# Up-projection of a two-layer encoder trunk as seven half-width products instead of eight, with the down-projection in groups of four

## The chip, the core and the metric

One core of a Trainium2 chip runs the whole program. The metric is device time in microseconds; the kernel before was timed three times (1096.11, 1097.59 and 1097.9 us, median 1097.59). One more execution was recorded by the profiler; all durations here come from that one.

## What is computed

Two layers (DEPTH = 2) over 512 positions of 1024 features. Each layer has an attention part and a channel mixer. The change is in the mixer:

```python
h = rms_norm(x, ffn_norm_g[i]) @ w_up[i]          # 1024 -> 2 x 2816
h = depthwise_conv(h, conv_w[i], conv_b[i])       # width 3 over positions
gate, up = jnp.split(h, 2, axis=-1)
x = x + (jax.nn.silu(gate) * up) @ w_down[i]      # 2816 -> 1024
```

## The kernel before

Everything is held feature-major: tiles have 128 features on the partitions and the 512 positions along the free dimension. Products keep fp32 accuracy by splitting each factor into a rounded part (hi) and a remainder (lo) and adding three TensorE products, hi·hi, hi·lo and lo·hi (`mm3`, lines 259 to 262). Weights stream through `WStream`: a chunk of 128x1024 is loaded by SyncE into one of 4 raw buffers; ScalarE writes the rounded half (line 123) and the negated chunk (line 125); a DMA issued by GpSimd (line 126) adds the chunk to that, which leaves the remainder. Six split buffers hold the results; the stream splits 3 plan entries ahead of use and loads 6 ahead.

In the mixer the 22 "pairs" j are 128 gate columns and the matching 128 value columns. `up(j)` (line 648) runs 2 x 8 x 3 = 48 matmuls of 512 columns into two PSUM banks, upg and upv. The rms factor of the positions is applied afterwards: after pair 0 the row statistics are summed on TensorE (`row_rsqrt`, line 232), VectorE computes the inverse root in small steps, and in the middle of pair 1 `row_broadcast` (line 248) spreads it over the partitions; ScalarE copies it out as rb (line 250). Only then can `up_post` (line 664) of pair 0 run: VectorE multiplies each bank by rb (line 670), ScalarE forms the middle tap (672), VectorE adds the outer taps (673 and 675), ScalarE the SiLU (678), VectorE the product (679), and the result g is split (683, 684). `down(g)` (line 687) multiplies a group of finished pairs by w_down, 24 matmuls of 512 columns for each pair, and VectorE adds each bank to x (709). Groups have 8, 8, 4 and 2 pairs (`ffn_order`); the last two stand at the end.

The framework orders each engine's queue once, when the program is built; at run time every queue is strictly in order, and an instruction that waits holds up all behind it. Tiles come from pools with a fixed number of buffers, so a full pool is a wait too.

Of the kernel before, what the change touches and what calls it, by code (L numbers as in the profile page):

```python
# [17 lines left out]
P = 128  # L18
# [6 lines left out]
NH = 8  # L25
# [4 lines left out]
GROUPS = [8, 8, 4, 2]  # L30
GCOLS = [256, 256, 512, 1024]
RAW_BUFS, SPL_BUFS, K8_BUFS, K2_BUFS = 4, 6, 8, 25
# [17 lines left out]
def ffn_order():  # L50
    order = []
    ng = len(GROUPS)
    for g in range(ng):
        lo = sum(GROUPS[:g])
        for j in range(lo, lo + GROUPS[g]):
            order.append(("up", j))
            if g > 0 and j == lo + 1 and g < ng - 1:
                order.append(("dn", g - 1))
    order.append(("dn", ng - 2))
    order.append(("dn", ng - 1))  # L60
    return order


def chunk_plan():
    plan = []
    for l in range(DEPTH):
# [6 lines left out]
        for kind, i in ffn_order():  # L73
            if kind == "up":
                plan += [(("up", l, i, h), 1024) for h in range(2)]
            else:
# [9 lines left out]
class WStream:  # L86
    def __init__(self, nc, wdram, raw_pool, split_pool, ahead_load, ahead_split):
        self.nc, self.w = nc, wdram
        self.raw_pool, self.split_pool = raw_pool, split_pool
# [9 lines left out]
    def chunk(self, i):  # L99
        o, n = self.offs[i] * P, PLAN[i][1]  # L100
        return self.w[o:o + n * P].rearrange("(p n) -> p n", p=P)

    def load_to(self, n):
        while self.loaded < min(n, len(PLAN)):
            i = self.loaded
            n_el = PLAN[i][1]
            t = self.raw_pool.tile([P, CH], F32, name="wraw")
            self.nc.sync.dma_start(out=t[:, 0:n_el], in_=self.chunk(i))
            self.raw[i] = t
            self.loaded += 1  # L110

    def split_to(self, n):
        nc = self.nc
        while self.split < min(n, len(PLAN)):
            i = self.split
            key, n_el = PLAN[i]
            raw = self.raw.pop(i)
            t = self.split_pool.tile([P, 2, CH], F32R, name="wspl")
            pieces = 2 if i == 0 else 1
            st = n_el // pieces  # L120
            for a in range(0, n_el, st):
                e = slice(a, a + st)
                nc.scalar.activation(out=t[:, 0, e], in_=raw[:, e], func=AF.Copy)  # L123
                if key[0] in DMA_LO:
                    nc.scalar.activation(out=t[:, 1, e], in_=raw[:, e], func=AF.Copy, scale=-1.0)  # L125
                    nc.gpsimd.dma_start(out=t[:, 1, e].bitcast(F32), in_=raw[:, e], accum_op=ALU.add)  # L126
                    continue
                lo = nc.gpsimd if key[0] in POOL_LO else nc.vector
                lo.tensor_tensor(out=t[:, 1, e], in0=raw[:, e], in1=t[:, 0, e].bitcast(F32), op=ALU.subtract)
            self.spl[i] = t  # L130
# [18 lines left out]
DMA_LO = ("vv", "u", "a2", "ws", "so", "ao", "up", "dn")  # L149
# [3 lines left out]
def trunk_kernel(ctx: ExitStack, tc: tile.TileContext, xT, wts, pk, gq, rope, out):  # L153
# [6 lines left out]
    splp = ctx.enter_context(tc.tile_pool(name="splp", bufs=SPL_BUFS))  # L160
    k8p = ctx.enter_context(tc.tile_pool(name="k8p", bufs=K8_BUFS))
# [25 lines left out]
    ws = WStream(nc, wts, rawp, splp, ahead_load=AHEAD_LOAD, ahead_split=AHEAD_SPLIT)  # L187
# [79 lines left out]
    for l in range(DEPTH):  # L267
# [98 lines left out]
        qt = [None, None]  # L366
        qs = [None] * NH

        def q_stacks(pi, bank):
            for par in range(2):  # L370
                h = 2 * pi + par
                if h % 4 == 0:
                    qt[h // 4] = k8("qs", F32R)
                a, o = (lohalf, hihalf) if par == 0 else (hihalf, lohalf)
                st = qt[h // 4][:, h % 4]
# [4 lines left out]
        def k_stacks(bank):  # L380
            kt_ = k8("kk", F32R)
            res = []
            for par in range(2):
                a, o = (lohalf, hihalf) if par == 0 else (hihalf, lohalf)
                kh, kl = kt_[:, 2 * par], kt_[:, 2 * par + 1]
# [8 lines left out]
        def vv_stat():  # L394
            vvg = vvx["g"]
            ss = tn(NT * NH, "ssv")
            for b in range(NT):
                sq = k2("sq")
                A.activation(out=sq, in_=vvg[:, b], func=AF.Square)
# [6 lines left out]
        def vv_norm(b):  # L406
            vvg, rs, vh, vl = vvx["g"], vvx["r"], vvx["h"], vvx["l"]
            V.tensor_tensor(out=vvg[:, b].rearrange("p (h d) -> p h d", h=NH), in0=vvg[:, b].rearrange("p (h d) -> p h d", h=NH),
                            in1=rs[:, b * NH:(b + 1) * NH].unsqueeze(2).to_broadcast([P, NH, HD]), op=ALU.mult)
            G.tensor_tensor(out=vvg[:, b], in0=vvg[:, b], in1=sgn_bc, op=ALU.mult)  # L410
            A.activation(out=vh[:, b], in_=vvg[:, b], func=AF.Copy)
# [48 lines left out]
        def scores(h, b):  # L460
# [13 lines left out]
            pt[b] = p  # L474

        ats = []
        att = [None]
        asq = [None]
        pair = []

# [333 lines left out]
```

## Time and profile before

| | us |
|---|---|
| median of three runs | 1097.59 |
| profiled execution, its time | 1096.55 |
| its span | 1094.8 |
| TensorE (PE) busy | 1079.2 (99%) |
| ScalarE (ACT) busy | 657.0 (60%) |
| VectorE (DVE) busy | 602.5 (55%) |
| GpSimd (POOL) busy | 282.0 (26%) |

The mixer of layer 1 fills about 191 to 550 us of the span, that of layer 2 about 731 to 1093 us. A busy time is the sum of the durations of an engine's instructions; successive ones overlap a little, so the distance from start to start of two neighbours is what a queue of them costs. In the rows below "idle" is how long an engine stood still just before an instruction, and the arrow names what it waited for. The profile's lines number the kernel before; in the changed kernel the same code stands about 45 to 130 lines further down.

### The profile page before, as it was taken

The page shows a single profiled execution, that of the slowest core. Times are in us where ns is not written, and L with a number is a line of the kernel's source. Part 1 is how long each engine was busy: PE and PEld are TensorE (multiplying, and loading weights), DVE is VectorE, ACT ScalarE, POOL GpSimd, SP SyncE. Part 2 cuts the span into 40 slices and gives each one's busy share as a digit, 9 for nine tenths or more (in the row PEclk, how much of TensorE's full clock was granted, in tenths as well). Part 3 has the DMA queues.
Part 4 walks back from the last instruction along what each step waited for, and adds up shares of the span by engine and source line. Part 5 has one row for each costly group of instructions (what it writes and reads, how often), then busy time and mean ns, then how long its engine had stood idle before and what let it go on. Part 6 is the DMA issues. An engine that isn't in the chain of part 4 may idle for free.

```text
span 1094.8 us, 13707 instructions
## 1 busy us (share of the span) xinstructions
PE 1079.2 (99%) x5024; PEld 896.8 (82%) x5024; DVE 602.5 (55%) x1068; ACT 657.0 (60%) x928; POOL 282.0 (26%) x335
## 2 busy tenths in 40 slices
PE   8989999999999999999999999999999999999998
PEld 7868888888888888888888878888888888888887
DVE  6678996565521555125647799866545134541353
ACT  7579786666644665346366896686665446563550
POOL 6434623311111111111063444251111111111110
PEclk9999999999999999999999999999999999999999
DMA  7985317888888888887668650377878787878762
GB/s 261 256 206 122 71 22 174 209 206 184 205 187 200 183 201 186 199 188 197 165 158 201 153 134 21 74 189 187 205 197 189 201 190 195 194 197 198 186 140 77
DMA packets 53923, 188.94 MB, mean 173 GB/s; under 512 B 6112, under 2 KB 6752, under 8 KB 53856
## 3 DMA queue, kind: packets, MB, share of 16 engines
q0 software_dynamic: 24480, 89.14, 45.2%
q1 hardware_dynamic: 29088, 98.79, 25.7%
q8 instruction: 39, 0.64, 0.2%
q14 instruction: 28, 0.23, 0.1%
q10 hardware_dynamic: 288, 0.14, 0.0%
HBM read 96.82 MB, written 2.10 MB: 90 GB/s over the span
## 4 chain that ended last, share of the span: by engine, by line
PE 90%; ACT 3%; DVE 3%; issue 1%; POOL 1%; DMA 0%; SPq 0%; DVEq 0%; ACTq 0%; POOLq 0%
PE upg L260 7%; PE upv L261 7%; PE upg L262 7%; PE upg L261 7%; PE upv L262 7%; PE dn L260 7%; PE dn L262 7%; PE upv L260 7%; PE dn L261 7%; PE a L260 1%; PE a L261 1%; PE a L262 1%; PE pT L490 1%; PE ao L261 1%; PE ao L262 1%
## 5 line engine op out<-in xcount | busy, mean ns | idle before, releaser
L126 POOL DMA_DIRECT2D wspl<-wraw x170 | 146.9, 866 | 669.1 <-ACT wspl L125 376.7
L123 ACT ACTIVATE wspl<-wraw 128x1024 fp32r<-128x1024 f32 (+1 forms) x179 | 188.6, 1053 | 203.0 <-issue 57.5
L125 ACT ACTIVATE wspl<-wraw 128x1024 fp32r<-128x1024 f32 x170 | 177.9, 1046 | 0.0
L260 PE MATMUL upg<-xh,wspl 128*128 128x512 f32 x352 | 137.2, 390 | 0.0
L262 PE MATMUL upg<-xh,wspl 128*128 128x512 f32 x352 | 137.0, 389 | 0.0
L262 PE MATMUL upv<-xh,wspl 128*128 128x512 f32 x352 | 137.0, 389 | 0.0
L261 PE MATMUL upv<-xl,wspl 128*128 128x512 f32 x352 | 137.0, 389 | 0.0
L262 PE MATMUL dn<-g,wspl 128*128 128x512 f32 x352 | 137.0, 389 | 0.0
L260 PE MATMUL upv<-xh,wspl 128*128 128x512 f32 x352 | 137.0, 389 | 0.0
L261 PE MATMUL upg<-xl,wspl 128*128 128x512 f32 x352 | 137.0, 389 | 0.0
L261 PE MATMUL dn<-g,wspl 128*128 128x512 f32 x352 | 137.0, 389 | 0.0
L260 PE MATMUL dn<-g,wspl 128*128 128x512 f32 x352 | 136.9, 389 | 0.0
L709 DVE TENSOR_TENSOR x<-x,dn 128x512 f32<-128x512 f32 x63 | 43.0, 686 | 155.3 <-PE dn L262 155.3
L672 ACT ACTIVATE ht<-ht,pk_sb 128x512 f32<-128x512 f32 x88 | 70.6, 807 | 67.8 <-DVE ht L670 67.8
L673 DVE SCALAR_TENSOR_TENSOR ht<-ht,pk_sb 128x511 f32<-128x511 f32 x88 | 65.9, 751 | 81.1 <-ACT ht L672 81.1
L670 DVE TENSOR_TENSOR ht<-upv,rb 128x512 f32<-128x512 f32 x44 | 30.4, 691 | 87.5 <-PE upv L262 87.2
L261 PEld LDWEIGHTS upv<-xl,wspl 128*128 128x128 f32 x352 | 66.1, 188 | 13.8
L262 PEld LDWEIGHTS upg<-xh,wspl 128*128 128x128 f32 x352 | 66.0, 188 | 13.8
L260 PEld LDWEIGHTS upg<-xh,wspl 128*128 128x128 f32 x352 | 66.2, 188 | 13.7
L262 PEld LDWEIGHTS upv<-xh,wspl 128*128 128x128 f32 x352 | 66.1, 188 | 13.7
L262 PEld LDWEIGHTS dn<-g,wspl 128*128 128x128 f32 x352 | 66.1, 188 | 13.7
L261 PEld LDWEIGHTS dn<-g,wspl 128*128 128x128 f32 x352 | 66.1, 188 | 13.7
(199 smaller groups left out, 2009.2 us busy)
## 6 DMA issues: line engine op xcount, KB each, us to landing
wraw<-in_wts SPq DMA_DIRECT2D x177, 512.0 KB, 4.3
wspl<-wraw POOLq DMA_DIRECT2D x170, 512.0 KB, 5.0
x<-in_xT SPq DMA_DIRECT2D x8, 256.0 KB, 6.1
out_y<-x SPq DMA_DIRECT2D x7, 256.0 KB, 2.0
wraw<-in_wts SPq DMA_DIRECT2D x2, 256.0 KB, 3.9
sgn<-in_gq SPq DMA_DIRECT2D x2, 256.0 KB, 4.5
rope<-in_rope SPq DMA_DIRECT2D x2, 256.0 KB, 4.0
pk_sb<-in_pk SPq DMA_DIRECT2D x1, 208.0 KB, 7.2
```

The source lines that it names most:

```text
L123: nc.scalar.activation(out=t[:, 0, e], in_=raw[:, e], func=AF.Copy)
L125: nc.scalar.activation(out=t[:, 1, e], in_=raw[:, e], func=AF.Copy, scale=-1.0)
L126: nc.gpsimd.dma_start(out=t[:, 1, e].bitcast(F32), in_=raw[:, e], accum_op=ALU.add)
L260: T.matmul(out, lhsT=lh, rhs=rh, start=start, stop=False)
L261: T.matmul(out, lhsT=lh, rhs=rl, start=False, stop=False)
L262: T.matmul(out, lhsT=ll, rhs=rh, start=False, stop=stop)
L490: T.transpose(bank[:, b * P:(b + 1) * P], pt[b][:, s * P:(s + 1) * P], ident)
L670: V.tensor_tensor(out=h, in0=banks[i], in1=rb[0], op=ALU.mult)
L672: A.activation(out=tt, in_=h, func=AF.Identity, scale=col(PK_CW + 2 * NCT + ct), bias=col(PK_CB + ct))
L673: V.scalar_tensor_tensor(out=tt[:, 1:S], in0=h[:, 0:S - 1], scalar=col(PK_CW + ct), in1=tt[:, 1:S], op0=ALU.mult, op1=ALU.add)
L709: V.tensor_tensor(out=x_sb[dt], in0=x_sb[dt], in1=bank, op=ALU.add)
```

## The change

Pairs 0 and 1 stay plain. From pair 2 on the gate and value columns of a pair, the even and odd feature tiles, and the first and second half of the positions form a 2 x 2 x 2 block product, done by a Strassen scheme in seven products of half width instead of eight. A product is 4 feature tiles x 3 matmuls = 12 matmuls of 256 columns.

The right factors (`side`, for all four tile pairs kp) are built once in each layer out of the normalised x, by sums and differences of halves, each split into hi and lo: 28 tiles of 128x512. The weight factors are built for each pair from two raw chunks: four sums or differences of 128x512 on VectorE (new lines 153, 154, 155 and 163), then the splits, of which that of chunk A has its remainder made by VectorE (141) instead of by the DMA, and the fourth factor's too. Work on a pair is in four stages on TensorE: A and B (two products each, into the halves of one bank), C (one product added to the half bank of A) and D (two products into the bank of B); the order is C(j), A(j+1), D(j), B(j+1). Shared sums come from ScalarE copies `pc` of banks A and B, taken before C and D write into them again, and from five 128x256 additions on VectorE.

The down-projection has groups of 4, 4, 4, 4, 4 and 2 pairs; the first four run between pairs, the last two at the end. Many four-in-one tiles become single ones (8 and 25 buffers become 3 and 45), two buffers for weight sums are added, and GpSimd's DMA scratch is set to 8192 bytes.

```diff
-GROUPS = [8, 8, 4, 2]
-GCOLS = [256, 256, 512, 1024]
-RAW_BUFS, SPL_BUFS, K8_BUFS, K2_BUFS = 4, 6, 8, 25
+GROUPS = [4, 4, 4, 4, 4, 2]
+GCOLS = [512, 512, 512, 512, 512, 1024]
+J0 = 2
+RAW_BUFS, SPL_BUFS, CMB_BUFS, K8_BUFS, K2_BUFS = 4, 6, 2, 3, 45
...
+            if key[0] == "upA":
+                r0, r1 = self.raw.pop(i)
+                lo, hi = slice(0, 512), slice(512, 1024)
+                c = self.cmb_pool.tile([P, CH], F32, name="wcmb")
+                V.tensor_tensor(out=c[:, lo], in0=r0[:, lo], in1=r0[:, hi], op=ALU.subtract)
+                V.tensor_tensor(out=c[:, hi], in0=r0[:, hi], in1=r1[:, hi], op=ALU.add)
+                V.tensor_tensor(out=r0[:, hi], in0=c[:, hi], in1=r0[:, lo], op=ALU.subtract)
+                self.pair[key[1:]] = (r0, r1, c)
+                self.spl[i] = self.halves(r0, slice(0, CH), key)
+            elif key[0] == "upB":
+                self.spl[i] = self.halves(self.pair[key[1:]][2], slice(0, CH), key)
+            elif key[0] == "upC":
+                r0, r1, _ = self.pair.pop(key[1:])
+                s4 = self.k2("s4")
+                V.tensor_tensor(out=s4, in0=r1[:, 0:512], in1=r0[:, 512:1024], op=ALU.subtract)
+                four = self.halves(s4, None, key, out=(self.k2("s4h", F32R), self.k2("s4l", F32R)), dma=False)
+                self.spl[i] = (self.halves(r1, slice(0, CH), key), four)
...
                 if j == 1 and n == KT - 1:
                     rb[0] = row_broadcast(rf[0])
-                    up_post(0, held[0])
+                    up_post(0, scaled(held[0]))
+                    for kp in range(KT // 2):
+                        side(kp)
...
+        def side(kp):
+
+            e, o = k2("zx"), k2("zx")
+            for t, d in ((e, 2 * kp), (o, 2 * kp + 1)):
+                V.scalar_tensor_tensor(out=t, in0=x_sb[d], scalar=col(PK_FN + d), in1=rb[0], op0=ALU.mult, op1=ALU.mult)
+            ta, tb = k2("zt"), k2("zt")
+            V.tensor_tensor(out=ta[:, lo2], in0=e[:, lo2], in1=e[:, hi2], op=ALU.subtract)
+            G.tensor_tensor(out=ta[:, hi2], in0=o[:, lo2], in1=e[:, lo2], op=ALU.subtract)
+            V.tensor_tensor(out=tb[:, lo2], in0=o[:, lo2], in1=ta[:, lo2], op=ALU.subtract)
+            G.tensor_tensor(out=tb[:, hi2], in0=o[:, hi2], in1=tb[:, lo2], op=ALU.subtract)
+            u = unit("ze")
+            parts = [(e[:, hi2], u[:, lo2], u[:, hi2])] + [(t, unit("zh"), unit("zl")) for t in (o, ta, tb)]
+            for t, h, w in parts:
+                A.activation(out=h, in_=t, func=AF.Copy)
+                V.tensor_tensor(out=w, in0=t, in1=h.bitcast(F32), op=ALU.subtract)
...
+        def product(out, hi, lo, z, first, last):
+            for kp in range(KT // 2):
+                sl = slice(kp * P, (kp + 1) * P)
+                rh, rl = Z[kp][z]
+                for n, (w, r) in enumerate(((hi, rh), (hi, rl), (lo, rh))):
+                    T.matmul(out, lhsT=w[:, sl], rhs=r, start=first and kp == 0 and n == 0,
+                             stop=last and kp == KT // 2 - 1 and n == 2, skip_group_check=True)
...
+        def stage(kind, j):
+            if kind in "AB":
...
+                product(bank[:, lo2], w[:, 0, 0:512], w[:, 1, 0:512], p0, True, False)
+                product(bank[:, hi2], w[:, 0, 512:1024], w[:, 1, 512:1024], p1, False, True)
+                c = k2("pc")
+                A.activation(out=c, in_=bank, func=AF.Copy)
...
+            elif kind == "C":
...
+                product(bank[:, lo2], w[:, 0, 0:512], w[:, 1, 0:512], "B21", False, True)
+                val = pairs[j]["val"] = k2("h")
+                A.activation(out=val[:, hi2], in_=bank[:, lo2], func=AF.Copy)
...
+                product(bank[:, lo2], w[:, 0, 512:1024], w[:, 1, 512:1024], "T4", False, False)
+                product(bank[:, hi2], four[0], four[1], "B22", False, True)
+                V.tensor_tensor(out=p["gate"][:, hi2], in0=bank[:, lo2], in1=u[:, lo2], op=ALU.add)
+                V.tensor_tensor(out=p["val"][:, lo2], in0=bank[:, hi2], in1=u[:, lo2], op=ALU.add)
+                up_post(j, [p["gate"], p["val"]])
```

Three places show what stands in a queue before and now. The first is VectorE in layer 1 from the spread of the row factor to the end of pair 0 (diag is the input of the spread, ht and g the tiles of `up_post`, L709 the multiplication by rb that was L670). Before:

```order
L246 TENSOR_TENSOR diag<-ident,rl 128x512
L670 TENSOR_TENSOR ht<-upg,rb 128x512
L670 TENSOR_TENSOR ht<-upv,rb 128x512
L673 SCALAR_TENSOR_TENSOR ht<-ht,pk_sb 128x511 x2
L675 SCALAR_TENSOR_TENSOR ht<-ht,pk_sb 128x511 x2
L679 TENSOR_TENSOR ht<-ht 128x512
```

Now (the z tiles are the right factors, zx the normalised x, zt the sums, wcmb and wraw weight sums of a later pair):

```order
L801 SCALAR_TENSOR_TENSOR ht<-h,pk_sb,ht 128x511 x2
L155 TENSOR_TENSOR wraw<-wcmb,wraw 128x512
L805 TENSOR_TENSOR ht<-ht 128x512
L808 TENSOR_TENSOR g<-ht,g 128x512
L732 SCALAR_TENSOR_TENSOR zx<-x_89,pk_sb,rb 128x512
L732 SCALAR_TENSOR_TENSOR zx<-x_90,pk_sb,rb 128x512
L734 TENSOR_TENSOR zt<-zx 128x256
L742 TENSOR_TENSOR z<-zx,z 128x256
L736 TENSOR_TENSOR zt<-zx,zt 128x256
L742 TENSOR_TENSOR z<-zx,z 128x512
```

All of pair 0's epilogue stands ahead of the first instruction of `side`; the 32 instructions of the four calls follow, and only behind them the multiplications of pair 1.

The second place is TensorE at the end of pair 1 in the same layer. Before, pair 2 follows at once:

```order
L260 MATMUL upv<-xh,wspl 128x512
L261 MATMUL upv<-xl,wspl 128x512
L262 MATMUL upv<-xh,wspl 128x512
L260 MATMUL upg<-xh,wspl 128x512
L261 MATMUL upg<-xl,wspl 128x512
L262 MATMUL upg<-xh,wspl 128x512
```

Now the stages A and B of pairs 2 and 3 are interleaved by tile pair kp, each matmul with a z tile:

```order
L305 MATMUL upv<-xh,wspl 128x512
L306 MATMUL upv<-xl,wspl 128x512
L307 MATMUL upv<-xh,wspl 128x512
L755 MATMUL uA<-z,wspl 128x256 x3
L755 MATMUL uB<-z,wspl 128x256
L755 MATMUL uA<-z,wspl 128x256 x5
L755 MATMUL uB<-z,wspl 128x256 x5
```

The order's count of these is 56 matmuls that stand ahead of the one that needs the last tile of `side`, and 66 from there to the first matmul of C of pair 2.

The third place is ScalarE between two down-projections of layer 1, around the copies pc of banks A and B (h<-uA is the copy after stage C, L798 the middle taps, L804 the SiLU, L807 the rounded g, L136 and L138 weight copies). Before, one pair:

```order
L672 ACTIVATE ht<-ht,pk_sb 128x512
L125 ACTIVATE wspl<-wraw 128x1024
L683 ACTIVATE g<-ht 128x512
L672 ACTIVATE ht<-ht,pk_sb 128x512
L123 ACTIVATE wspl<-wraw 128x1024
L678 ACTIVATE ht<-ht 128x512
L125 ACTIVATE wspl<-wraw 128x1024
L123 ACTIVATE wspl<-wraw 128x1024
```

Now, one pair:

```order
L782 ACTIVATE h<-uA 128x256
L766 ACTIVATE pc<-uA 128x512
L798 ACTIVATE ht<-h,pk_sb 128x512 x2
L804 ACTIVATE ht<-ht 128x512
L807 ACTIVATE g<-ht 128x512
L766 ACTIVATE pc<-uB 128x512
L136 ACTIVATE wspl<-wraw 128x1024
L136 ACTIVATE wspl<-wcmb 128x1024
L136 ACTIVATE s4h<-s_4005 128x512
L138 ACTIVATE wspl<-wcmb 128x1024
```

The copy of bank B stands behind the whole epilogue of the pair before, and TensorE's stage D waits for that copy.

## Rows read from the trace of the kernel before

**Rows 1.** The page, busy time, share of the span and instructions of each engine
```profile
PE 1079.2 (99%) x5024; PEld 896.8 (82%) x5024; DVE 602.5 (55%) x1068; ACT 657.0 (60%) x928; POOL 282.0 (26%) x335
```

**Rows 2.** Windows: stretch, its length, busy by engine, granted clock, DMA share, GB/s
```profile
300.00:400.00 100.00, 100.00 (x443) 82.84 (x442) 34.99 (x49) 51.42 (x59) 16.19 (x19) 1.00 0.81 193
```

**Rows 3.** Timeline of TensorE: start, duration; 25 matmuls of 512 columns, first and last
```profile
299.95 0.39 PE L261 MATMUL upv<-xl,wspl 128*128 128x512 f32 x1
...
305.39 0.39 PE L261 MATMUL dn<-g,wspl 128*128 128x512 f32 x1
```

**Rows 4.** Timeline of TensorE: 18 and 16 matmuls of 256 columns, first and last
```profile
93.14 0.28 PE L260 MATMUL a<-wspl,xh 128*128 128x256 f32 x1
...
95.16 0.28 PE L262 MATMUL a<-wspl,xl 128*128 128x256 f32 x1
...
88.51 0.28 PE L262 MATMUL mix<-vh,wspl 128*128 128x256 f32 x1
...
90.31 0.28 PE L262 MATMUL mix<-vh,wspl 128*128 128x256 f32 x1
```

**Rows 5.** Timeline of TensorE around pair 1 of layer 1
```profile
208.11 0.63 PE L248 MATMUL ps<-diag,ones_r 128*128 128x512 f32 x2
...
213.81 0.39 PE L262 MATMUL upv<-xh,wspl 128*128 128x512 f32 x1
214.04 0.39 PE L260 MATMUL upg<-xh,wspl 128*128 128x512 f32 x1
```

**Rows 6.** Timeline of VectorE there, with idle time before and its releaser
```profile
205.97 0.68 DVE L246 TENSOR_TENSOR diag<-ident,rl 128x512 fp32r<-128x512 f32 x1
209.46 0.69 DVE L670 TENSOR_TENSOR ht<-upg,rb 128x512 f32<-128x512 f32 x1 [2.81 <-ACT rb L250]
210.07 0.68 DVE L670 TENSOR_TENSOR ht<-upv,rb 128x512 f32<-128x512 f32 x1
211.04 1.46 DVE L673 SCALAR_TENSOR_TENSOR ht<-ht,pk_sb 128x511 f32<-128x511 f32 x2 [0.29 <-ACT ht L672]
212.41 1.41 DVE L675 SCALAR_TENSOR_TENSOR ht<-ht,pk_sb 128x511 f32<-128x511 f32 x2
...
217.06 0.69 DVE L684 TENSOR_TENSOR g<-ht,g 128x512 fp32r<-128x512 f32 x1 [0.18 <-ACT g L683]
```

**Rows 7.** Timeline of ScalarE there
```profile
210.19 1.52 ACT L672 ACTIVATE ht<-ht,pk_sb 128x512 f32<-128x512 f32 x2 [0.76 <-DVE ht L670]
211.62 1.05 ACT L123 ACTIVATE wspl<-wraw 128x1024 fp32r<-128x1024 f32 x1
212.57 1.04 ACT L125 ACTIVATE wspl<-wraw 128x1024 fp32r<-128x1024 f32 x1
213.63 1.28 ACT L678 ACT_TABLE_LOAD   x1
214.92 0.63 ACT L678 ACTIVATE ht<-ht 128x512 f32<-128x512 f32 x1
```

**Rows 8.** Groups of VectorE by form: count, busy us, mean ns, idle before and releaser
```profile
L706 DVE TENSOR_TENSOR x<-x,dn 128x256 f32<-128x256 f32 x2 | 0.8, 418 | 0.7 <-PE dn L262 0.7
L709 DVE TENSOR_TENSOR x<-x,dn 128x512 f32<-128x512 f32 x63 | 43.0, 686 | 155.3 <-PE dn L262 155.3
```

**Rows 9.** The same groups in 200 to 550 us: a subtraction of 128x1024
```profile
L129 DVE TENSOR_TENSOR wspl<-wraw,wspl 128x1024 fp32r<-128x1024 f32 x4 | 4.9, 1222 | 3.5 <-ACT wspl L123 3.5
```

**Rows 10.** Timeline of VectorE, the same addition beside GpSimd's and alone
```profile
178.16 1.28 DVE L619 TENSOR_TENSOR x<-x,aot 128x512 f32<-128x512 f32 x1
...
181.89 0.69 DVE L619 TENSOR_TENSOR x<-x,aot 128x512 f32<-128x512 f32 x1
```

**Rows 11.** Timeline of GpSimd there
```profile
177.59 1.30 POOL L227 TENSOR_TENSOR sqacc<-sqacc,sq 128x512 f32<-128x512 f32 x1 [1.08 <-ACT sq L226]
```

**Rows 12.** Groups of TensorE by form: 128-column matmuls at the start and later
```profile
L490 PE MATMUL pT<-ident,p 128*128 128x128 f32 x256 | 34.0, 274 | 2.9 <-ACT p L471 1.9 <-POOL p L473 0.7
...
L207 PE MATMUL warmup<-ones 128*128 128x128 f32 x16 | 3.8, 431 | 1.1 <-DVE warm L183 1.1
```

More of the change, by code (lines that the diff above doesn't have):

```diff
@@ L50, in ffn_order @@
 def ffn_order():
-    order = []
+    order = [("c", j) for j in range(J0)]
     ng = len(GROUPS)
[L53 to L58, printed above, removed]
+    ends = {sum(GROUPS[:g + 1]) - 1: g for g in range(ng)}
+    order += [("A", J0), ("B", J0)]
+    for j in range(J0, NCT):
+        order.append(("C", j))
+        if j + 1 < NCT:
+            order.append(("A", j + 1))
+        order.append(("D", j))
+        if j + 1 < NCT:
+            order.append(("B", j + 1))
+        g = ends.get(j - 1)
+        if g is not None and g < ng - 2:
+            order.append(("dn", g))
     order.append(("dn", ng - 2))
@@ L116, in split_to @@
             key, n_el = PLAN[i]
[L117 to L129, printed above, removed]
@@ L130, in split_to @@
-            self.spl[i] = t
+            if key[0] == "upA":
[15 more added lines that the diff above has]
+                self.spl[i] = (self.halves(r1, slice(0, CH), key), four)
+            else:
+                raw = self.raw.pop(i)
+                pieces = 2 if i == 0 else 1
+                st = n_el // pieces
+                t = self.split_pool.tile([P, 2, CH], F32R, name="wspl")
+                for a in range(0, n_el, st):
+                    e = slice(a, a + st)
+                    self.halves(raw[:, e], e, key, out=(t[:, 0, e], t[:, 1, e]))
+                self.spl[i] = t
@@ L661, in up, with scaled, unit @@
             else:
-                up_post(j, banks)
-        def up_post(j, banks):
+                up_post(j, scaled(banks))
+        def scaled(banks):
+            hs = []
+            for bank in banks:
+                hs.append(k2("h"))
+                V.tensor_tensor(out=hs[-1], in0=bank, in1=rb[0], op=ALU.mult)
+            return hs
+        lo2, hi2 = slice(0, 256), slice(256, 512)
+        zunits = []
+        def unit(name):
+            n = len(zunits)
+            if n < 4 * K8_BUFS:
+                if n % 4 == 0:
+                    zk8.append(k8("z", F32R))
+                u = zk8[-1][:, n % 4]
+            else:
+                u = k2(name, F32R)
+            zunits.append(u)
+            return u
@@ L722, in trunk_kernel @@
         for kind, i in ffn_order():
-            if kind == "up":
-                up(i)
+            if kind == "c":
+                up_plain(i)
+            elif kind == "dn":
+                down(i)
             else:
-                down(i)
+                stage(kind, i)
 def host_arrays(x, attn_norm_g, w_in, q_norm_g, k_norm_g, sg_norm_g, sg_w, sg_b,
@@ L769, in host_arrays @@
         assert a.shape == (P, n_el)
-        parts.append(a.reshape(-1))
+        parts += [a[:, c:c + CH].reshape(-1) for c in range(0, n_el, CH)]
     wts = np.concatenate(parts)
```

144 lines of the change are left out of this document (93 added, 51 removed).

## The prediction, made before the changed kernel was timed

> **What bounds the kernel now.** I read the page's busy times first, then windows of the mixer, then timelines of single queues. TensorE is busy for 1079.2 of 1094.8 us [rows 1], and in 100 us of the mixer it never stops, at a granted clock of 1.00, while VectorE has 35.0 and ScalarE 51.4 us of work [rows 2]. A TensorE-bound kernel gets faster by what TensorE no longer does, as long as nobody makes it wait. So there are two questions: what a half-width matmul costs, and where the new VectorE and ScalarE work comes to lie in front of TensorE.
>
> **What TensorE saves.** From the first to the last of 25 matmuls of 512 columns there are 24 steps in 5.44 us, 0.2267 us each [rows 3]. Of 256 columns there are 17 steps in 2.02 us, 0.1188 us, in the attention part, and 15 in 1.80 us, 0.120 us, in the gating [rows 4]; both kinds load new weights for each matmul, as the change does. A pair falls from 48 x 0.2267 = 10.88 us to 84 x 0.1188 = 9.98 us: 0.90 us, not the eighth (1.36) that the columns promise, because the smaller matmul is dearer per column. Over 20 pairs and 2 layers: **-36.0 us**; with 0.120 us it is -32. The down-projection keeps its matmuls; its additions to x rise from 32 to 48 a layer, but VectorE stands idle 155.3 us in front of these [rows 8], so they cost nothing.
>
> Against this stands a formula. In the trace 512 columns cost 0.2267 and 256 cost 0.1188 us [rows 3, 4]. The Trainium skill ("TensorE: Matmul & The Clock Gate", section "Back-to-back issue gap") gives a warm gap of N/2.4 + 2.5 ns, 215.8 and 109.2 ns, an estimate by which the pair would save 1.19 us and the change 47 us. The rows differ from it at both widths, so the rows decide.
>
> **What `side` costs, in each layer.** Its input rb exists only in the middle of pair 1. Before, the spread starts on TensorE at 208.11, VectorE has rb at 209.46, and pair 1's last matmul makes way for pair 2 at 214.04 [rows 5, 6]. Diag was ready 1.5 us ahead of its matmul (205.97 + 0.68 against 208.11). Now two instructions of the weight sums stand among the inverse root's small steps: one of 128x512 (0.61 us, the step 209.46 to 210.07 [rows 6]) and one of 128x1024 (1.22 us [rows 9]). Together they eat the lead and 0.3 to 1 us more: TensorE waits **0.5 us**, and pair 1 ends at 214.5.
>
> VectorE then does all of pair 0's epilogue before `side`, as the first place of the order shows. Two multiplications and two weight sums are 4 x 0.61 = 2.4 us, the outer taps (211.04 to 212.41 for two) 2.7 us; product and g wait for ScalarE's table load (1.28 us), SiLU (0.63) and the copy of g, as they did before [rows 6, 7]. Before, g began at 217.06 with no weight sums ahead but with one multiplication of pair 1; I take 217.1 as the time at which `side` starts. It is 8 instructions of 512 with a scalar at 0.69 (the step 211.04 to 212.41, halved), 12 of 512 at 0.61 and 12 of 256 at 0.34 (mean 418 ns [rows 8] less the 0.08 by which neighbours overlap): 5.5 + 7.3 + 4.1 = 16.9 us, plus 0.7 for hand-offs to ScalarE and back. GpSimd does 8 sums of 128x256 meanwhile. An addition of two SBUF tiles took 1.28 us beside such a GpSimd instruction and 0.69 alone [rows 10, 11]; each of the 8 then adds 0 to 0.5 us, and I take 2 us in all. So `side` ends at 217.1 + 16.9 + 0.7 + 2 = 236.7 (234 to 239).
>
> TensorE can't be kept busy from 214.5 to 236.7: its order has 56 matmuls ahead of the one that needs the last tile, 56 x 0.1188 = 6.7 us. It is idle 22.2 - 6.7 = **15.5 us** (12.8 to 17.8). This is the main term.
>
> Behind `side` VectorE owes pair 1's epilogue: two multiplications, a 128x1024 subtraction, four taps, product and g, 1.2 + 1.2 + 2.7 + 1.2 = 6.4 us, with ScalarE's part and three weight copies of 0.95 [rows 7] in between. ScalarE's copies of banks A and B of pair 2 stand behind that, some 8.7 us after `side`, and stage C waits for the first; TensorE has 66 matmuls (7.8 us) to bridge it, which leaves 0.9. Following the queues on in the same way, ScalarE's weight copy for A of pair 5 stands behind pair 2's epilogue and comes 2.9 us late. I take **4 us** (0 to 7). Nothing in this trace shows TensorE starved for 20 us, so what its clock does is unknown: 0 to 4 us, and I take **1**, since the 56 matmuls keep it partly busy.
>
> Sum for a layer 0.5 + 15.5 + 4 + 1 = 21 us; for two **+42 us**.
>
> **The later stretches.** Between two down-projections stand four pairs of pure up-projection, 10.0 us of TensorE each. VectorE's share of such a pair rises from 5.2 us (two multiplications, four taps, product, g) to 9.9: less the multiplications, plus five sums of 512 and 1024 for the weights, five additions of 256, and the fourth factor's remainder. ScalarE's rises from 6.3 to 9.1 (five weight copies at 0.95, one of 512, two and a half bank copies, the epilogue's four). Both fit, barely; the down-projection's 21.8 us lets them catch up, but only as far as six split buffers allow. What decides is the queue: D of a pair waits for the bank copy of its B, which stands on ScalarE behind the epilogue of the pair before (third place of the order). From the end of one D to the next, TensorE has some 60 matmuls, 7.1 us. The chain in that time is two additions of 256 (0.7), two taps on ScalarE (1.43 [rows 7]), the third outer tap done 1.4 later, SiLU 0.6, product 0.6, g 0.6, bank copy 0.6: about 6.3 us with the hand-offs. One weight copy in the chain fits, two don't. Walking one stretch through, two of its four D come 0.8 us late. So 1.5 us for each of 8 stretches: **+12 us** (0, if the copies fall beside waits, to 32, if each of 32 pairs pays a copy).
>
> The attention part keeps its matmuls; their order moves around the gating's output products, and the tile pools change. I take nothing for it, with 3 us either way. The smaller DMA scratch can only delay GpSimd's issues, which have 5 us a chunk; nothing.
>
> **The sum.** 1096.55 - 36 + 42 + 12 = 1114.5 us for the profiled execution; the median was 1.0 us above it, so **1115 us**, 1.6% slower.
>
> **The rivals.** *Faster (the other side).* The mechanism is the same stall, at its small end: GpSimd costs VectorE nothing, the backlog hides under the 66 matmuls and under the first down-projection, and the later copies slip between waits. A layer then pays 12.8 + 0.5, and the sum is 1097.6 - 36 + 26.6 = 1088. It decides in favour of faster once all stalls together stay under 18 us a layer. For it speaks that VectorE and ScalarE have half their time free on average [rows 1]; against it that 12.8 us follow from VectorE's own instructions, with no wait counted.
>
> *ScalarE and VectorE become the bound of the stretches.* If each pair runs at 11 us instead of 10, because raw buffers come free late (two are now held until the third split of a pair) and the copies queue, the later term is 40 us instead of 12: 1143. For it speaks 9.9 and 9.1 us of work in 10; against it the pause in each down-projection.
>
> *The clock falls.* In this trace the clock was low only at the start: a 128-column matmul took 431 ns there and 274 later [rows 12]. If it falls to 1.2 GHz in the gap of `side`, half-width matmuls should cost about what full-width ones do now, 0.227: the 66 behind the gap then take 7.1 us longer in each layer, and with the 1 already counted the sum is 1115 + 12 = 1127. The Trainium skill (the same page, section "HAM oscillation — how this bites in real kernels") says that waits between bursts of matmuls do this; no row before shows it.
>
> **How the numbers follow.** The forecast's case, stalls above the saving, has 0.62; the faster rival 0.15, and 0.08 lies within 0.2% of 1097.6 (about 2.2 us, what a measurement can tell); the bound stretches 0.10, the clock 0.05. So slower 0.77. The range takes the unknown ends in turn: low 1095, where `side` costs 13 to 15 us a layer, the backlog 2 and the stretches 3 in all; high 1138, with a gap of 17.8, a backlog of 7 and half the price of the bound stretches.
>
> **What would show it.** Right: in both layers VectorE goes without pause through the zx, zt and z instructions for 17 to 22 us, and TensorE's idle time in front of uA and uB is 10 us or more in each; 256-column matmuls start 0.119 us apart elsewhere; small waits of D for ScalarE's bank copy. Wrong: an idle time in front of uA under 8 us a layer (the order of the queue didn't hold VectorE as I read it), matmuls at 0.13 us or more, or waits for weights (split tiles, raw loads) larger than those for `side`.

## The result and the profile after

The changed kernel took 1269.99 us (median of 4 runs, 1267.28 to 1271.74) beside 1097.24 us of the kernel before on the same chip: ratio 1.157, 95% interval 1.155 to 1.160. The forecast of 1115 us had the sign and was 155 us too low; the time lies far above the range.

The page of the profiled execution (1269.72 us, span 1267.9), busy times and granted clock in 40 slices, to be laid beside [rows 1]:

```profile
PE 1114.8 (88%) x6464; PEld 978.4 (77%) x6464; DVE 848.1 (67%) x1524; ACT 776.3 (61%) x1160; POOL 297.7 (23%) x351
...
PEclk9999997689899898989999999986898989979899
```

TensorE should have been busy for 36 us less and is busy for 36 us more, and it also stands idle. Summed over the timeline of TensorE from 60 us on, its idle time rose from 8 to 145 us. Matmuls that started more than 0.119 us (256 columns) or 0.2267 us (512) apart, with no idle time between them, lost 7 us before and 64 now. Where TensorE waits, its groups of waits say (who waits, for what, us in all, times, longest):

```profile
PE uB L755 <- ACT pc L766: 76.8, 8, 11.1
PE dn L307 <- DMA wspl<-wraw: 11.8, 10, 2.5
PE uA L755 <- ACT z L741: 10.5, 4, 4.9
PE uA L755 <- ACT wspl L136: 9.3, 2, 5.0
```

The first line is eight waits of 9 to 11 us: one in each of the eight later stretches. `pc` is ScalarE's copy of a bank. Windows of layer 1 (stretch, length, busy by engine in the order PE, PEld, DVE, ACT, POOL, then granted clock, DMA share, GB/s): two such stretches with the down-projection between them, then 20 us around the wait of the second:

```profile
316.00:369.60 53.60, 42.47 (x338) 42.08 (x337) 32.85 (x55) 33.88 (x47) 7.75 (x9) 0.90 0.67 151
369.60:392.50 22.90, 22.04 (x98) 17.92 (x97) 12.30 (x21) 10.70 (x14) 2.59 (x3) 1.00 0.76 199
392.50:444.80 52.30, 42.73 (x337) 42.32 (x336) 33.54 (x56) 34.22 (x47) 7.75 (x9) 0.90 0.71 157
404.00:408.00 4.00, 3.30 (x28) 3.09 (x26) 0.00 (x0) 0.00 (x0) 0.00 (x0) 1.00 0.89 204
408.00:412.00 4.00, 0.00 (x0) 0.00 (x0) 3.46 (x6) 2.50 (x4) 0.00 (x0) 0.82 0.35 70
412.00:416.00 4.00, 0.00 (x0) 0.00 (x0) 3.20 (x6) 3.20 (x5) 0.86 (x1) 0.50 0.14 28
416.00:420.00 4.00, 3.54 (x16) 3.55 (x17) 3.03 (x6) 3.69 (x6) 0.86 (x1) 0.50 0.84 131
420.00:424.00 4.00, 4.00 (x33) 4.00 (x32) 1.90 (x4) 1.52 (x2) 0.00 (x0) 0.90 0.89 226
```

Four pairs are 40 us of matmuls, and the eight stretches take 52 to 55 each. From 404 to 408 VectorE, ScalarE and GpSimd have nothing to do, while the DMA engines are busy: as the queues below show, a load is awaited. Then TensorE stops, its granted clock falls to 0.50 (1.2 GHz), and half-width matmuls start 0.213 us apart (15 steps in 3.20 us from 417.26 on) instead of 0.120 (26 in 3.12 us up to 406.90). The Trainium skill ("TensorE: Matmul & The Clock Gate", section "HAM oscillation — how this bites in real kernels") tells of DMA waits between bursts of matmuls that lower the clock each time; the trace agrees: 0.50 after the stop of 9.2 us here, and after the stop of 9.0 to 11.1 us in each of the other seven stretches.

Who is late, read through the queues (GpSimd, the load's issue by SyncE, VectorE, ScalarE, TensorE; start, duration, line, what it does, idle time before and releaser):

```profile
396.84 0.86 POOL L139 DMA_DIRECT2D wspl<-wraw  x1 [1.55 <-ACT wspl L138]
...
402.51 0.33 SPq L122 DMA_DIRECT2D wraw<-in_wts  x1
...
401.52 0.68 DVE L833 TENSOR_TENSOR x<-x,dn 128x512 f32<-128x512 f32 x1
408.00 0.69 DVE L154 TENSOR_TENSOR wcmb<-wraw 128x512 f32<-128x512 f32 x1 [5.80 <-DMA wraw<-in_wts]
408.73 0.69 DVE L155 TENSOR_TENSOR wraw<-wcmb,wraw 128x512 f32<-128x512 f32 x1
...
401.12 1.06 ACT L138 ACTIVATE wspl<-wraw 128x1024 fp32r<-128x1024 f32 x1
409.50 1.06 ACT L136 ACTIVATE wspl<-wraw 128x1024 fp32r<-128x1024 f32 x1 [7.32 <-issue]
410.46 1.50 ACT L798 ACTIVATE ht<-h,pk_sb 128x512 f32<-128x512 f32 x2
...
415.29 0.63 ACT L807 ACTIVATE g<-ht 128x512 fp32r<-128x512 f32 x1 [0.77 <-DVE ht L805]
415.82 0.58 ACT L766 ACTIVATE pc<-uB 128x512 f32<-128x512 f32 x1
...
416.45 1.01 PE L755 MATMUL uB<-z,wspl 128*128 128x256 f32 x3 [9.16 <-ACT pc L766]
```

Stage D (416.45) waits for the bank copy pc (415.82). TensorE had left that bank at 402.6, but in ScalarE's queue the copy stands behind the epilogue of the pair before (410.46 to 415.29), and that behind a weight copy (409.50) which waits for VectorE's weight sums (408.00), which wait for a raw load. The load was late because its buffer was: a pair holds two of the four raw buffers, and the second comes free only when the DMA that adds the chunk to its negated copy (the accumulate DMA of C's split) has read it. That DMA was issued at 396.84; with the page's median of 5.7 us from issue to landing (last column below) it ends at 402.5. The load was issued at 402.51 and let VectorE go on at 408.00, after 5.5 us, where the median is 4.9:

```profile
wraw<-in_wts SPq DMA_DIRECT2D x177, 512.0 KB, 4.9
wspl<-wraw POOLq DMA_DIRECT2D x130, 512.0 KB, 5.7
```

### The profile page after: what moved, and what is told of

The parts are those of the page before. It is cut to its first block, busy times and chain, and to the rows that moved or that the text cites. A ratio compares the mean times of both kernels' runs of the same rounds, so it can differ in the third digit from the quotient of the medians.

```text
span 1267.9 us, 17453 instructions
## 1 busy us (share of the span) xinstructions
PE 1114.8 (88%) x6464; PEld 978.4 (77%) x6464; DVE 848.1 (67%) x1524; ACT 776.3 (61%) x1160; POOL 297.7 (23%) x351
## 4 chain that ended last, share of the span: by engine, by line
PE 40%; DMA 19%; DVE 15%; issue 15%; ACT 10%; POOL 0%; SPq 0%; POOLq 0%; DVEq 0%; ACTq 0%
DMA wspl<-wraw 9%; DMA wraw<-in_wts 9%; PE uB L755 8%; PE uA L755 6%; PE dn L307 3%; PE dn L306 3%; PE dn L305 3%; ACT wspl L136 2%; ACT ht L798 2%; ACT wspl L138 1%; DMA wspl<-wcmb 1%; DVE m L510 1%; PE a L306 1%; PE a L305 1%; DVE pl L534 1%
## 5 line engine op out<-in xcount | busy, mean ns | idle before, releaser
L136 ACT ACTIVATE wspl<-wraw 128x1024 fp32r<-128x1024 f32 (+1 forms) x179 | 187.9, 1050 | 240.1 <-issue 77.5
L755 PE MATMUL uB<-z,wspl 128*128 128x256 f32 x600 | 106.5, 304 | 83.6 <-ACT pc L766 76.8
L755 PEld LDWEIGHTS uB<-z,wspl 128*128 128x128 f32 x600 | 90.1, 207 | 89.0 <-ACT pc L766 78.6
L138 ACT ACTIVATE wspl<-wraw 128x1024 fp32r<-128x1024 f32 x130 | 136.5, 1050 | 0.0
L755 PE MATMUL uB<-zh,wspl 128*128 128x256 f32 x560 | 131.1, 300 | 0.0
L755 PE MATMUL uA<-z,wspl 128*128 128x256 f32 x600 | 98.9, 293 | 22.9 <-ACT z L741 10.5
L755 PEld LDWEIGHTS uA<-z,wspl 128*128 128x128 f32 x600 | 85.4, 199 | 27.0 <-ACT z L741 11.9
L755 PEld LDWEIGHTS uB<-zh,wspl 128*128 128x128 f32 x560 | 105.3, 210 | 0.0
L307 PEld LDWEIGHTS dn<-g,wspl 128*128 128x128 f32 x352 | 66.5, 189 | 29.9 <-DMA wspl<-wraw 16.3
L755 PE MATMUL uA<-zh,wspl 128*128 128x256 f32 x400 | 86.9, 286 | 0.0
L798 ACT ACTIVATE ht<-h,pk_sb 128x512 f32<-128x512 f32 x88 | 66.6, 805 | 30.4 <-DVE h L788 28.8
L755 PE MATMUL uB<-zl,wspl 128*128 128x256 f32 x280 | 84.3, 301 | 0.2
L306 PEld LDWEIGHTS dn<-g,wspl 128*128 128x128 f32 x352 | 66.7, 189 | 13.8
L305 PEld LDWEIGHTS dn<-g,wspl 128*128 128x128 f32 x352 | 66.7, 190 | 13.2
L833 DVE TENSOR_TENSOR x<-x,dn 128x512 f32<-128x512 f32 x95 | 64.4, 681 | 16.7 <-PE dn L307 16.7
```

The lines of the kernel that those rows point to most:

```text
L136: nc.scalar.activation(out=hi, in_=src, func=AF.Copy)
L138: nc.scalar.activation(out=lo, in_=src, func=AF.Copy, scale=-1.0)
L305: T.matmul(out, lhsT=lh, rhs=rh, start=start, stop=False)
L306: T.matmul(out, lhsT=lh, rhs=rl, start=False, stop=False)
L307: T.matmul(out, lhsT=ll, rhs=rh, start=False, stop=stop)
L755: T.matmul(out, lhsT=w[:, sl], rhs=r, start=first and kp == 0 and n == 0, stop=last and kp == KT // 2 - 1 and n == 2, skip_group_check=True)
```

## The experiments

Theory A: this loop over the raw buffers sets the stretches, and the falling clock adds to its waits. Rivals: B or Q, ScalarE's and VectorE's queues are too full or in a bad order whatever the loads do; the sums of x are the main loss; groups and pools cost by themselves. All ratios are to the kernel before, timed beside each run. To make room, some runs (e1, e5 to e7, e10 to e13) have 41 small scratch buffers instead of 45, and e14 has 43. The runs stand here by what they tell, not in the order in which they were made.

**e3: all pairs plain.**

```diff
-J0 = 2
+J0 = 22
-                    for kp in range(KT // 2):
-                        side(kp)
```

(and down-projections placed among plain pairs as before)

> All 22 pairs of both layers are plain, as before the change; kept of the change are groups of four in the down-projection, the new pool sizes, single scratch tiles, the smaller DMA scratch and the new layout of the up weights. If the half products with their weight handling are the whole loss, the time is within 1% of the kernel before, 1095 to 1110 us (the two attention parts were 3.7 and 5.1 us longer in the changed kernel, which pool sizes could explain). If groups of four cost by themselves (more down-projection weights tiles of 512 columns and more additions into x), 1115 to 1150 us.

1106.28 us, ratio 1.0085 (1.007 to 1.010). The two mixers take 360.6 us each, as before; groups of four cost nothing. The attention parts are 4.2 and 5.1 us longer than before.

**e14: the same with the old DMA scratch.**

```diff
-RAW_BUFS, SPL_BUFS, CMB_BUFS, K8_BUFS, K2_BUFS = 4, 6, 2, 3, 45
+RAW_BUFS, SPL_BUFS, CMB_BUFS, K8_BUFS, K2_BUFS = 4, 6, 1, 3, 43
-    ..., num_devices=1, dynamic_dma_scratch_size=8192)
+    ..., num_devices=1)
```

> The run with all pairs plain (1106.3 us, mixers as long as before, the two attention parts 4.3 and 5.1 us longer), with the DMA scratch size of before (43 small scratch buffers and one of the unused sum buffers fewer make the room). If the scratch size makes the attention parts longer: 1097 to 1099 us. If it is the scratch pools (single tiles instead of blocks of four): 1105 to 1108 us.

1105.26 us, 1.0073 (1.006 to 1.009). It is not the DMA scratch: what is left of the change in the attention parts is the tile pools and the weights' layout, and the waits that are new there are for tiles that the pool change touches:

```profile
PE pv L546 <- ACT ph L539: 3.0, 2, 1.5
...
PE pT L536 <- DVE pl L540: 2.4, 2, 1.2
```

Pools and layout were not tried apart.

**e7: one up weight tile for all half products.** It leaves out all loads, sums, splits and accumulate DMAs of these weights but one tile a layer.

```diff
+            if key[0] in ("upA", "upB", "upC"):
+                if self.kept[l] is None:
+                    self.halves(self.raw.pop(i), None, key, out=(w[:, 0], w[:, 1]))
+                    self.kept[l] = w
+                w = self.kept[l]
+                self.spl[i] = (w, (w[:, 0, 0:512], w[:, 1, 0:512])) if key[0] == "upC" else w
```

> Left out: all handling of the up-projection weights from the third pair on: one tile is loaded and split per layer and stands in for all of them (no further loads, sums, splits, accumulate DMAs); the matmuls, the sums of x, the sums of products, the conv and the down-projection stay. What remains over the ideal (before, less 36 us of TensorE, plus 9 us of the attention parts: 1070 us) is then the sums of x and the output's sums. Theory A and Q alike (the loss sits in the weights' path): 1095 to 1130 us. If the products' own chain (bank copy, sums, conv on ScalarE and VectorE) bounds a pair above TensorE's 10.0 us: over 1160 us.

1107.6 us, 1.0105 (1.009 to 1.012). A later stretch now takes what its matmuls take, so neither the bank copies nor the conv steps bound it by themselves; the first one, with the sums of x, takes longer (windows, columns as above):

```profile
223.30:267.50 44.20, 38.90 (x276) 36.49 (x277) 35.33 (x58) 20.33 (x34) 8.34 (x9) 0.91 0.22 48
292.60:332.90 40.30, 40.30 (x337) 40.26 (x337) 20.81 (x38) 17.60 (x28) 1.73 (x2) 1.00 0.25 63
```

From e3 to e7 TensorE saves 36 us by the prediction's count and the time grows by 1.3: the sums of x cost 37 us, if that count holds. Even with weights for nothing this scheme, placed like this, is no faster than plain pairs, and 11 us slower than before, 9 of which e3 has too.

**e12: the same with the half products from the fifth pair on.**

```diff
-J0 = 2
+J0 = 4
```

> The run with one up weight tile (left out: loads, sums, splits and accumulate DMAs of the up-projection weights from the first half product on; 1107.6 us), with the half products from the fifth pair on. There each layer's mixer took as long as before (361 against 360.5 us), so the 18 us that TensorE saves per layer went elsewhere, by the traces to the wait for the sums of x and the low clock after it. If so, two plain pairs ahead of the first use hide them: 1107.6 - 2 x 18 + 2 x 1.8 = 1075 us, up to 1085. If the sums of x only move their cost onto the conv steps of these pairs: 1095 to 1105 us.

1087.76 us, 0.9924 (0.991 to 0.994), a little above the 1075 to 1085 expected. It is 20 us less than e7, though four pairs fewer are halved (3.6 us). Two plain pairs hide most of the sums of x, and the granted clock stays up:

```profile
PE 1058.5 (97%) x6320; PEld 932.8 (86%) x6320; DVE 675.6 (62%) x1274; ACT 580.9 (54%) x926; POOL 234.4 (22%) x279
...
PEclk9999999999999999999999999999999999999999
```

The mixers take 352.9 and 352.2 us, 8 under those before, of 16 saved in each; the attention parts, 7 us longer together, take almost half of that back. So with the weights' path free the scheme gives 0.8% as tried here; what it gives with the pools of before was not tried.

**e6: the up weights loaded once.** The raw tiles of each layer's third pair serve all later ones; only the later loads are left out.

```diff
+            if PLAN[i][0][0] == "upA":
+                if l not in self.kept:
+                    self.kept[l] = [self.pin.tile([P, CH], F32, name=f"wpin{a}") for a in range(2)]
...
+                self.raw[i] = self.kept[l]
+                continue
```

> Left out: the loads of the up-projection weights from the fourth pair on; the two raw tiles of a layer's third pair stay in buffers of their own and every later pair makes its sums and splits from them, so all work on VectorE, ScalarE, GpSimd and the accumulate DMAs stays, and only loads and the waits for raw buffers go. Theory A: the stretch waits (77 us before uB) go, and with them most of the 56 us by which the matmuls are slower than at full clock: 1140 to 1185 us. Theory Q (queue load and order): the waits stay, 1225 to 1270 us.

1152.85 us, 1.0511 (1.050 to 1.053): 117 us less than the changed kernel, with all VectorE, ScalarE and GpSimd work in place. The waits for pc are gone from the head of TensorE's list:

```profile
PE uB L766 <- DMA wspl<-wcmb: 14.5, 11, 1.9
PE uA L766 <- ACT z L752: 10.1, 4, 4.8
...
PE uB L766 <- ACT pc L777: 4.6, 3, 2.0
```

Theory A's range held, theory Q's did not: full queues alone don't make the long waits. By TensorE's timeline 86 of the 117 us are idle time and 26 low clock. But the framework orders the queues anew for each kernel, and in e6 the last 46 matmuls of a stretch stand behind the first of the down-projection; the bank copy still stands behind the epilogue. So the 117 us are those of the loads together with the order that came with them. No run holds the order fixed: e2, e4 and e8 stay close to the changed kernel's, while e1 differs on VectorE and ScalarE, and e5, e6, e9, e10 and e13 on TensorE too.

**e13: the same, remainders by VectorE instead of the accumulate DMAs.**

```diff
-DMA_LO = ("vv", "u", "a2", "ws", "so", "ao", "up", "dn", "upB", "upC")
+DMA_LO = ("vv", "u", "a2", "ws", "so", "ao", "up", "dn")
```

> The run whose up-projection weights were loaded once (left out: all later loads of them; 1152.9 us), with the remainders of the second and third tile of a pair made by VectorE instead of the accumulate DMAs: 40 x 2 subtractions of 1.25 us more on VectorE (100 us, which brings it to some 945 us of work), 80 copies of 1.05 us less on ScalarE. The run with one tile and no handling took 1107.6 us, so sums, splits and accumulate DMAs cost 45 us. If the accumulate DMAs' latency (5 us, the waits for the second tile before uB) is that: 1115 to 1135 us. If it is work on the two in-order queues: 1150 us or more.

1150.35 us, 1.048 (1.046 to 1.050). So the 45 us between e6 and e7 do not go when the accumulate DMAs go: either these were not the cause, or the VectorE work in their place (it is busy for 928 us now, 846 in e6) costs as much. Which part of the sums and splits makes them stays open.

**e8: no sums of x.** The half products take halves of the plain split tiles of x; the sums and their splits are left out.

```diff
-            e, o = k2("zx"), k2("zx")
-            ...
+            e, o = xs[2 * kp], xs[2 * kp + 1]
```

> Left out: the sums of x and their splits; the half products take halves of the plain split tiles of x instead (same shapes, other numbers), all weight handling stays. The stretch from the start of the up-projection to the end of the third pair is some 20 us longer per layer in the changed kernel than 33 us of work; if the sums of x are that, 1225 to 1240 us, with the eight waits in the later stretches unchanged at 9 to 11 us. If they are the main loss: below 1200 us.

1226.58 us, 1.1179 (1.115 to 1.121): 43 us less, 21.7 a layer, at the edge of what was expected. The later waits for pc stay (10.8, 9.1, 9.6 and 9.8 us in layer 1).

**e4: half products from the fifth pair on**, all else as changed.

```diff
-J0 = 2
+J0 = 4
```

> The half products begin with the fifth pair instead of the third; the sums of x are made at the same place, so two plain pairs (some 22 us of TensorE work) lie between them and their first use. Four of 40 pairs go back to plain, which costs 4 x 0.9 = 3.6 us of TensorE. If the sums of x are the main loss (the 21 us per layer of the prediction or more), the gap before the first half product closes and the time falls by 30 to 45 us, to 1225 to 1240 us. By theory A the sums cost only the gaps seen around them, about 5 + 6 us per layer, and two stretches of eight get no shorter: 1240 to 1260 us.

1240.13 us, 1.1301 (1.128 to 1.132). On the border of the two expectations, so alone it tells nothing apart; its waits do: the gap before the first uA is gone, and the waits for pc in the stretches are 9.3 to 11.0 us as ever.

**e1: six raw buffers; e2: the third tile's remainder by VectorE; e5: both.**

```diff
-RAW_BUFS, SPL_BUFS, CMB_BUFS, K8_BUFS, K2_BUFS = 4, 6, 2, 3, 45
+RAW_BUFS, SPL_BUFS, CMB_BUFS, K8_BUFS, K2_BUFS = 6, 6, 2, 3, 41
```

```diff
-DMA_LO = ("vv", "u", "a2", "ws", "so", "ao", "up", "dn", "upB", "upC")
+DMA_LO = ("vv", "u", "a2", "ws", "so", "ao", "up", "dn", "upB")
```

> Six raw weight buffers instead of four (paid for with 41 small scratch buffers instead of 45); nothing else differs from the changed kernel, 1270 us. Theory A (the loop over the raw buffers sets the stretches: a pair keeps two of the four until the accumulate DMA of its last third has landed, and the next load, the weight sums, the splits and the bank copy stand behind it in a row): a third pair's buffers are free, so the eight waits of 9 to 11 us before uB (76.8 us in the chain of waits of TensorE) fall below 3 us each and the granted clock rises with them: 1150 to 1190 us. Theory B (ScalarE's and VectorE's queues are simply too full in a stretch, whatever the loads do): the waits stay at 8 us or more, 1255 to 1280 us.

> The remainder of the third weight tile of a pair (C's) is made by VectorE instead of by ScalarE's negated copy and the accumulate DMA, so the raw buffer comes free some 5 us earlier with the same four buffers; ScalarE has one 1.2 us copy less per pair, VectorE one subtraction of about 1.2 us more, 40 pairs. Theory A (raw-buffer loop): each of the eight waits of 9 to 11 us shrinks by 4 to 7 us, and the clock rises: 1180 to 1230 us. Theory B for VectorE (its queue is the bound): 40 x 1.2 = 48 us more work there, 1275 to 1310 us. Theory B for ScalarE: 40 x 1.2 less there, 1225 to 1250 us, with the waits still on late raw loads gone from no place.

> The two earlier edits together: six raw weight buffers (41 small scratch buffers) and the remainder of a pair's third weight tile by VectorE. Each alone gave 30 us (1240.6 and 1239.2 us against 1270). Theory A (the loop over the raw buffers): with three pairs of buffers and no accumulate DMA on the second of them the loop has slack, no wait before uB in a later stretch is over 3 us, 1195 to 1220 us. Theory Q (VectorE's and ScalarE's queues are in order, and the weight sums and splits of the next pairs stand there behind the additions into x and the conv steps, so loads and buffers are not the limit any more): the gains do not add, 1225 to 1245 us.

1240.63, 1239.23 and 1212.67 us (ratios 1.130, 1.1298 and 1.1045; 1.099 to 1.110 for the last). Alone, e1 hit neither range, and e2 missed theory A's and fell into that of a ScalarE whose queue is too full (which e6 then speaks against as the cause of the long waits, its ScalarE being as busy as the changed kernel's, 776 us); together they come into A's range, though with waits up to 4.8 us where 3 were expected. In e2, which keeps nearly the changed kernel's order and has more VectorE work, the longest wait for pc falls from 11.1 to 4.9 us, as theory A would have it. The waits for pc in e1, then in e2:

```profile
PE uB L755 <- ACT pc L766: 64.8, 12, 8.9
```

```profile
PE uB L755 <- ACT pc L766: 33.2, 16, 4.9
```

With two more buffers the loop is wider, but the accumulate DMA also takes longer, 7.1 us to landing instead of 5.7; that more loads at a time are the reason is not shown:

```profile
wspl<-wraw POOLq DMA_DIRECT2D x130, 512.0 KB, 7.1
```

Theory Q may have its part here too: weight sums stand in VectorE's queue behind additions to x (`L833` above), which in the changed kernel waited 16.7 us in all for TensorE. No run tries this alone.

**e9: the third tile also split right behind the first; e10: six buffers on top; e11: and half products from the fifth pair on.**

```diff
                 self.spl[i] = self.halves(r0, slice(0, CH), key)
+                if PLAN[i + 2][0][0] == "upC":
+                    self.third(i + 2)
```

(`third` holds the lines that split C; e2's edit is in all three, e1's in the last two, J0 = 4 in the last)

> As the run with the third tile's remainder on VectorE (1239 us), and the third tile (with its fourth factor) is split right behind the pair's first tile instead of behind its second, in three pairs of four (not where a down-projection stands between). Four raw buffers, no other change. Theory A worked out: from one use of a raw buffer to the next there lie the first and second tile's splits and the copies between them (some 7 us), the third's split, the accumulate DMA (5.7), the load (5) and the sums (2), together 23 to 25 us for two pairs that TensorE does in 20; with VectorE's remainder 18 to 20, with the earlier split 12 to 14. So the waits before uB, 1 to 5 us each with VectorE's remainder alone, go below 1 us: 1195 to 1220 us. Theory Q (VectorE's queue is the limit now): 1230 us or more.

> The edit before with six raw buffers (41 small scratch buffers) on top. Theory A: the loop has slack already, and a third pair of buffers gives little, 0 to 15 us under the run before it. If loads are still late because of the queue ahead of the splits (theory Q), also little, but then both are above 1225 us.

> All edits that helped together: six raw buffers, third tile by VectorE and split early, and the half products from the fifth pair on, so that two plain pairs lie between the sums of x and their use. From the run before it the sums of x (some 18 us per layer in the run with one weight tile) should be partly hidden: 20 to 35 us less, 1165 to 1195 us; it is not expected to reach the kernel before, since with loads out of the way altogether the time was still 1153 us.

1219.92, 1191.22 and 1168.7 us (1.1128, 1.0874 and 1.067). e9 came at the top of its range with waits of 1 to 3 us left instead of the 0 to 1 expected; e10 took 29 us off where theory A gave 15 at most, so its arithmetic of a loop with slack is too simple; that late loads and queue order act on each other is a reading, not shown. In e10 the waits for pc are down to 2.6 us at the longest:

```profile
PE uB L762 <- ACT pc L773: 20.6, 12, 2.6
```

Every step that frees raw buffers sooner helped, and none reached the kernel before. e10 has 79 of the 117 us that e6 gives; where the other 38 come from stays open. Since e12 gives 0.8%, no further version was tried.

## Why the prediction was wrong, point by point

**What TensorE saves: right.** 26 half-width matmuls in 3.12 us are 0.120 us each at full clock, and in e12 half of the saving reaches the time of the mixers. The Trainium skill's gap formula ("TensorE: Matmul & The Clock Gate", section "Back-to-back issue gap"), which the page gives for a single matmul in isolation and not for a stream with weight loads as here, is again below what the rows show: 109.2 ns against 120.

**`side`: right in size, wrong in make-up.** 21 us a layer were forecast, e7 gives 18.7 (37 over two layers) and e8 21.7; that the size fits is partly luck. But the idle time forecast at 15.5 us is 10.1 in layer 1, the sum of nine waits before uA and uB of pairs 2 and 3, and the slow matmuls around it make up much of the rest. In e7, where only the sums of x disturb this part, TensorE is idle for 9.9 us there, and matmuls spaced wider than at full clock add some 6, where the prediction took 1 for the clock. Layer 1 of the changed kernel there:

```profile
231.17 1.41 DVE L732 SCALAR_TENSOR_TENSOR zx<-x,pk_sb,rb 128x512 f32<-128x512 f32 x2
...
232.71 0.38 PE L755 MATMUL uA<-z,wspl 128*128 128x256 f32 x1 [4.86 <-ACT z L741]
...
235.00:240.00 5.00, 4.04 (x15) 3.35 (x16) 5.00 (x9) 2.23 (x4) 2.88 (x4) 0.50 0.69 131
240.00:245.00 5.00, 2.88 (x10) 2.00 (x10) 4.82 (x8) 2.31 (x4) 1.84 (x3) 0.50 0.00 0
245.00:250.00 5.00, 3.46 (x13) 2.58 (x13) 4.90 (x9) 2.31 (x4) 1.48 (x3) 0.50 0.00 0
```

VectorE went through `side` without a pause, as forecast, in 21 us. But `side` starts at 231.17, not at 217.1: pairs 0 and 1 took 33.2 us instead of the 23.2 of the kernel before, which the prediction priced at 0.5. TensorE waited for x there too, because weight sums stand among VectorE's last steps of the attention part and wait for raw loads themselves, and ran at 0.50 from 210 to 215. In e7, without weight sums, the two pairs took 23.2, and in e6, with the sums but without the late loads, 23.2 as well (in an order of its own).

```profile
189.37 1.80 DVE L153 TENSOR_TENSOR wcmb<-wraw 128x512 f32<-128x512 f32 x1 [3.12 <-DMA wraw<-in_wts]
...
194.20 0.69 DVE L154 TENSOR_TENSOR wcmb<-wraw 128x512 f32<-128x512 f32 x1 [1.04 <-DMA wraw<-in_wts]
...
205.12 0.51 PE L305 MATMUL upg<-xh,wspl 128*128 128x512 f32 x1 [2.29 <-ACT xh L300]
...
210.00:215.00 5.00, 5.00 (x17) 4.23 (x17) 2.36 (x5) 3.47 (x4) 1.50 (x2) 0.50 0.35 113
```

**The later stretches: the step that failed.** +12 us (0 to 32) were forecast. The eight stretches take 426.9 us where e7's take 325.4: 101 us more. The whole weights' path is 162 (1270 against 1107.6); the first stretches, with `side`, have 26 of the rest, pairs 0 and 1 have 19. The walk through the queues was right in its last link, that D waits for pc behind the epilogue. It went wrong where it took every weight copy on ScalarE as 0.95 us of work with its input there: the copy waited 7.3 us for weight sums that waited for a load, and everything in order behind it waited too. The rival of the bound stretches named the raw buffers and priced it all at about one us a pair; it is 3.2 (101 over 32 pairs). The price was never worked out from the loop itself, though its parts, 4.3 us to landing for a load and 5.0 for an accumulate DMA, stood on the page of before:

```profile
wraw<-in_wts SPq DMA_DIRECT2D x177, 512.0 KB, 4.3
wspl<-wraw POOLq DMA_DIRECT2D x170, 512.0 KB, 5.0
```

**The clock: too low a chance.** The rival had 0.05 and 12 us, in the gap of `side` alone. It fell in all eight stretches as well. With `side` and the first pairs it cost some 48 us: the 64 of slow matmuls less the 16 that the same sum gives in e12, where the clock stays up. The prediction also says that the clock was low in the trace of before only at the start; it was not. It stood at 0.50 for 3.4 us from 80.9 on, after short waits (two windows of before, columns as above):

```profile
78.00:81.00 3.00, 1.23 (x5) 0.60 (x4) 1.62 (x3) 2.95 (x5) 0.65 (x1) 0.98 0.39 112
81.00:85.00 4.00, 3.57 (x13) 3.01 (x14) 3.47 (x6) 3.97 (x6) 0.21 (x1) 0.59 0.87 201
```

**Attention: 0 forecast, 9 measured** (e3; 8.8 in the changed kernel), outside the 3 either way. That the smaller DMA scratch costs nothing held (e14).

**The sum** by the runs: 1097 + 9 (pools) - 36 + 37 (sums of x) + 45 (sums and splits of weights) + 117 (loads) = 1269. These are differences from run to run in the order e3, e7, e6, so they must add up; taken from the other end, e8 gives 43 for the sums of x instead of 37. The sign came out right by luck: `side`, the main term of the forecast, only cancels the saving (37 against 36), and the 162 of the weights decide. The condition that the forecast gave for being wrong, waits for weights larger than those for `side`, is met. (The terms named for the upper end of its range add up to about 1134 and not 1138, which changes nothing.)

## What to carry to other kernels

Before new work is put on a weight stream, write down the loop of one buffer, from load through sums, splits and the last reader back to the next load, with its measured latencies, and compare it with the time in which the consumer uses up the buffers. Here a pair held two buffers of four until the last of its three splits, and a stream that had been hidden became the bound; six buffers, with the order that came with them, gave back 29 us. In an in-order queue one late load delays all that stands behind it: here a bank copy, with its input ready, that the bottleneck engine waited for.

## What was not expected of the hardware

At the granted clock of 0.50 half-width matmuls start 0.213 us apart, 1.8 times the 0.120 at full clock and not twice. The same accumulate DMA of 512 KB landed after a median of 5.7 us with four raw buffers and of 7.1 with six (e1; 6.3 in e5, which has six and 40 of these DMAs fewer).
